# A recorded trunk issued in a planned order, and one product's weights summed by accumulating loads

## The chip, the cores and the metric

The kernel runs on one core of a Trainium2 chip. The metric is the time of one execution on the device in microseconds (us): the median of several runs. A core has five engines that run their own instruction streams in order: PE (TensorE, matrix products), DVE (VectorE), ACT (ScalarE), POOL (GpSimd) and SP (SyncE, which here only issues transfers). Streams wait for one another by semaphores. Weights come from HBM by DMA, issued by SP (plain loads) and POOL (loads that add to what is in the tile).

## The reference, cut to what matters

Two layers on 512 tokens of width 1024, all in float32:

```python
for i in range(DEPTH):                       # 2
    hn = rmsnorm(h, mix_norm_g[i])
    if i % N_MIXERS == 0:
        h = h + sgu_mixer(hn, ...)           # W_o (u * (W_s LN(v) + b)), u, v = gelu(hn @ w_in)
    else:
        h = h + retention(hn, positions, ...) # 4 heads: rotary q, k; decayed causal scores; gated by silu(g)
    h = h + swiglu(rmsnorm(h, ffn_norm_g[i]), ffn_w_gu[i], ffn_w_down[i])   # hidden width 2816
return rmsnorm(h, final_norm_g)
```

The work is matrix products: `hn @ w_in`, the gate/up and down products of both layers, the four heads' q, k, v, g, scores and values, and the two output projections.

## The kernel before, in words

Every float32 operand is kept as a high and a low half, and each product is three matmuls (`three`, L246 to L249). The halves are made when they are needed: ACT copies the high half (L216), DVE subtracts it to get the low half (L223). Weights are fetched by SP (`load`, L346) or, adding, by POOL (`add`, L349); where two or three blocks of a weight matrix have to be summed, either POOL's adding loads do it, or DVE adds raw tiles (`plus`, L377).

Nearly all large products go through `seven`, a scheme of seven products instead of eight on 2 x 2 blocks, named P1, P7, P6, Q4, P5, P2 and P3, in an order given by ORDER, LATER, FIRST or SPREAD. Each accumulates into a PSUM tile named X, Y or Z (W for P3 of the last unit). For which products POOL's adding loads make the summed weights is the argument `dma`; `onto` names products whose weights are made by adding one more block onto the tile of the product before.

A PSUM tile is 128 x 2 x 512 floats: two halves of 512 columns. There are four such tiles (`PS`, tags ps0 to ps3), handed out in turn. The last product, P3, is computed half by half: all matmuls of half c = 0, then `evac(p, acc, 0)`, then all matmuls of half c = 1, then `evac(p, acc, 1)`, so that half 0 can be read on DVE or ACT while half 1 is still being computed:

```python
            elif n == len(steps) - 1:
                for c in range(2):
                    with tc.issue_after(mm.ins) if apart and c == 1 else nullcontext():
                        for st_ in steps[-by_chunk:]:
                            mm = matmuls(p, *st_, c)
                    evac(p, acc, c)
```

The readers of such halves that this text names are: the products `s` and `he` of the gate/up units (L1036, DVE), the sums into the residual X (L527, DVE), the gated `ur` (L969, DVE) and `mx` (L988, DVE) of the first mixer, the scores times decay `s` (L1182, DVE), and on ACT the activated `v` (L837), the gate `sg` (L1214), the squares `osq` (L1232), the turned `z` (L1247), the copies `xr` (L704) and `s_dn` (L539). In sc, pv, v and the like the two parts of one tile are filled and read one after the other in the same way. A gate/up unit u of layer l has tiles X_gu, Y_gu and Z_gu; the projection of values and gates of a retention head has X_vg, Y_vg and Z_vg; dn is a down projection, so and ro the output projections.

The stages are: the first mixer (v, u, mix, so), feed-forward of layer 0 (gate/up units 0 to 5, dn0_0, dn0_1), retention (qk and vg of heads 0 to 3, scores sc, values pv, zT, ro), feed-forward of layer 1, and the final norm. The down projection that ends the kernel, dn1_1, is the last unit: `into_x(..., apart=True)`.

The rotary tables (cos and sin of the positions, `rotary_tables`, L852 to L898) are a long row of small DVE operations, stepped through in gate/up unit 2 of layer 0; they are used where head 0's q and k are rotated (L1099, L1100).

What sets the order of the work: `pipeline` runs a list of jobs and calls the preparing steps of later jobs some jobs ahead (FETCH, HIGH, PREP and so on). Below that, the framework's scheduler (`schedule_with_timeline_sim=True`) may move an instruction of any engine ahead of others when it puts the streams together, and it knows `issue_after` and `high_priority`. The semaphores that it puts in follow whole tiles.

## Time and profile before

| | |
|---|---|
| runs, median (lowest to highest of 3) | 1202.37 us (1201.17 to 1203.57) |
| the profiled execution, its own time | 1203.41 us |
| its span in the profile | 1201.7 us |
| DMA | 225.90 MB, mean 188 GB/s |
| granted TensorE clock, whole span | 0.996 |

Rows of groups read: line, engine, operation, out<-in, partitions x elements, count, then busy us and mean ns of one, then the idle time of the engine just before them and what ended most of it. A wait of PE names what PE waited for. Matmuls are pipelined: one of 512 columns is shown as 0.39 us, but they start every 0.23 us.

### The profile page before, as it was taken

How to read it: one execution, taken by the hardware profiler on the slowest of the kernel's cores; microseconds unless marked ns; L12 is line 12 of the kernel's file. 1: busy time of each engine (PE TensorE's matmuls, PEld its weight loads, DVE VectorE, ACT ScalarE, POOL GpSimd, SP SyncE). 2: the span in 40 equal slices, each digit the busy share in tenths (PEclk: the TensorE clock that was granted, in tenths of full speed). 3: DMA queues.
4: the chain of work that ended last, by engine and by line, in shares of the span. 5: the costliest groups of instructions: out<-in, count | busy, mean ns of one | idle time of the engine just before them, and what ended most of it. 6: DMA issues, size and time to landing. Idle time of an engine off the chain costs nothing.

```text
span 1201.7 us, 18455 instructions
## 1 busy us (share of the span) xinstructions
PE 1180.0 (98%) x7374; PEld 1067.4 (89%) x7374; DVE 960.9 (80%) x1143; ACT 664.6 (55%) x842; POOL 171.0 (14%) x151
## 2 busy tenths in 40 slices
PE   8999999999999999999999999999999999999997
PEld 7888899989999987988989898878899989999986
DVE  5587998899977789787885959879788896676897
ACT  5523775554444547555664656566565545535465
POOL 1000122121010130110201111220121210101210
PEclk9999999999999999999999999999999999999999
DMA  9912878898684898777677868877868887856892
GB/s 314 282 47 59 244 161 182 226 228 208 160 205 108 225 184 265 176 163 184 155 202 178 192 155 203 183 151 247 217 153 211 186 216 210 199 135 192 168 245 97
DMA packets 128167, 225.90 MB, mean 188 GB/s; under 512 B 7464, under 2 KB 30032, under 8 KB 128080
## 3 DMA queue, kind: packets, MB, share of 16 engines
q1 hardware_dynamic: 88848, 153.37, 38.6%
q0 software_dynamic: 38944, 70.81, 35.3%
q8 instruction: 58, 0.95, 0.3%
q10 hardware_dynamic: 288, 0.52, 0.1%
q14 instruction: 29, 0.24, 0.1%
HBM read 221.53 MB, written 2.10 MB: 186 GB/s over the span
## 4 chain that ended last, share of the span: by engine, by line
PE 85%; DMA 5%; issue 4%; DVE 2%; ACT 2%; POOL 1%; SPq 0%; DVEq 0%; POOLq 0%; ACTq 0%
PE X_gu L247 6%; PE X_gu L249 6%; PE X_gu L248 6%; DMA wr_gu_P<-in_ffn_w_gu 3%; PE Y_gu L249 3%; PE Y_gu L248 3%; PE Y_gu L247 3%; PE X_dn L247 3%; PE X_dn L248 3%; PE X_dn L249 3%; PE X_vg L247 2%; PE X_vg L248 2%; PE X_vg L249 2%; PE ps_v L247 1%; PE Y_dn L248 1%
## 5 line engine op out<-in xcount | busy, mean ns | idle before, releaser
L216 ACT ACTIVATE wh_gu_P<-wr_gu_P 128x1024 fp32r<-128x1024 f32 x132 | 135.3, 1053 | 87.6 <-DVE wr_gu_P L377 51.0
L223 DVE TENSOR_TENSOR wl_gu_P<-wr_gu_P,wh_gu_P 128x1024 fp32r<-128x1024 f32 x132 | 158.7, 1219 | 25.4 <-ACT wh_gu_P L216 25.1
L349 POOL DMA_DIRECT2D wr_gu_P<-in_ffn_w_gu x50 | 60.9, 1258 | 414.0 <-DVE wl_gu_P L223 196.2
L216 ACT ACTIVATE wh_dn_P<-wr_dn_P 128x1024 fp32r<-128x1024 f32 x72 | 69.1, 980 | 42.6 <-DMA wr_dn_P<-in_ffn_w_down 17.8
L223 DVE TENSOR_TENSOR wl_dn_P<-wr_dn_P,wh_dn_P 128x1024 fp32r<-128x1024 f32 x72 | 79.4, 1128 | 2.7 <-issue 1.1
L223 DVE TENSOR_TENSOR wl_vg_P<-wr_vg_P,wh_vg_P 128x1024 fp32r<-128x1024 f32 x48 | 57.8, 1217 | 14.5 <-ACT wh_vg_P L216 14.4
L349 POOL DMA_DIRECT2D wr_dn_P<-in_ffn_w_down x36 | 41.9, 1239 | 143.6 <-DVE wl_dn_P L223 46.6
L216 ACT ACTIVATE wh_vg_P<-wr_vg_P 128x1024 fp32r<-128x1024 f32 x48 | 49.2, 1055 | 22.8 <-DMA wr_vg_P<-in_ret_w_in 16.7
L349 POOL DMA_DIRECT2D wr_vg_P<-in_ret_w_in x26 | 31.5, 1248 | 207.5 <-DMA wr_vg_P<-in_ret_w_in 73.8
L247 PE MATMUL X_gu<-XH_f,wh_gu_P 128*128 128x256 f32 x176 | 50.6, 288 | 2.2 <-ACT xr_f L704 2.2
L247 PE MATMUL Z_gu<-XH_f,wh_gu_P 128*128 128x256 f32 x176 | 50.0, 284 | 1.4 <-DVE s L1051 1.4
L247 PE MATMUL X_gu<-xP5h_f,wh_gu_P 128*128 128x256 f32 x176 | 50.0, 284 | 0.9 <-ACT u L1026 0.9
L249 PE MATMUL Y_gu<-XH_f,wl_gu_Q 128*128 128x256 f32 x176 | 49.9, 284 | 0.8 <-DVE wl_gu_Q L223 0.8
L248 PE MATMUL X_gu<-XL_f,wh_gu_P 128*128 128x256 f32 x176 | 50.5, 287 | 0.0
L249 PE MATMUL X_gu<-XH_f,wl_gu_P 128*128 128x256 f32 x176 | 50.5, 287 | 0.0
L247 PE MATMUL X_gu<-xP6h_f,wh_gu_P 128*128 128x256 f32 x176 | 50.0, 284 | 0.2
L247 PE MATMUL Y_gu<-XH_f,wh_gu_Q 128*128 128x256 f32 x176 | 49.9, 284 | 0.0
L249 PE MATMUL Z_gu<-XH_f,wl_gu_P 128*128 128x256 f32 x176 | 49.9, 283 | 0.0
L248 PE MATMUL X_gu<-xP6l_f,wh_gu_P 128*128 128x256 f32 x176 | 49.8, 283 | 0.0
L249 PE MATMUL X_gu<-xP3h_f,wl_gu_P 128*128 128x256 f32 x176 | 49.8, 283 | 0.0
L248 PE MATMUL X_gu<-xP3l_f,wh_gu_P 128*128 128x256 f32 x176 | 49.8, 283 | 0.0
L249 PE MATMUL X_gu<-xP6h_f,wl_gu_P 128*128 128x256 f32 x176 | 49.8, 283 | 0.0
(643 smaller groups left out, 4284.5 us busy)
## 6 DMA issues: line engine op xcount, KB each, us to landing
wr_gu_P<-in_ffn_w_gu SPq DMA_DIRECT2D x110, 512.0 KB, 5.3
wr_gu_P<-in_ffn_w_gu POOLq DMA_DIRECT2D x50, 512.0 KB, 7.8
wr_dn_P<-in_ffn_w_down SPq DMA_DIRECT2D x50, 512.0 KB, 5.5
wr_vg_P<-in_ret_w_in SPq DMA_DIRECT2D x40, 512.0 KB, 5.8
wr_dn_P<-in_ffn_w_down POOLq DMA_DIRECT2D x30, 512.0 KB, 7.3
wr_vg_P<-in_ret_w_in POOLq DMA_DIRECT2D x26, 512.0 KB, 6.9
wr_ro_P<-in_ret_w_out SPq DMA_DIRECT2D x20, 512.0 KB, 4.8
wr_qk_P<-in_ret_w_in SPq DMA_DIRECT2D x15, 512.0 KB, 5.9
```

Source lines behind the costliest of these rows:

```text
L216: nc.scalar.activation(h, s, AF.Copy)
L223: nc.vector.tensor_tensor(l, s, f32(h), ALU.subtract)
L247: nc.tensor.matmul(o, ah, bh, start=start, stop=False, skip_group_check=True)
L248: nc.tensor.matmul(o, ah, bl, start=False, stop=False, skip_group_check=True)
L249: return nc.tensor.matmul(o, al, bh, start=False, stop=stop, skip_group_check=True)
L349: nc.gpsimd.dma_start(raw[p, 0, g, s][:, 0:nk, :], source(b, g, s, nk), accum_op=ALU.add)
```

## The change

The trunk's instructions are no longer given to the framework's scheduler. Stand-ins for the engines, the pools and the tiles (`EngineProxy`, `Pool`, `Virtual`, `View`) record each call in a list with an estimated length, and with the recorded calls that it must follow. `order_of` then plans all engines' work in time, and `emit` issues the calls in the order of their planned starts under `tc.manual_schedule()`, in which the framework keeps the order it is given and only puts the semaphores in. PE's operations are taken in recorded order as soon as they may run (the lowest number that is ready); DVE, ACT, POOL and SP take, of what may run, the one whose latest start is earliest (`late`, from a backward pass). `issue_after` and `high_priority` no longer do anything.

Which calls must follow which is kept in grains: 512 floats (`BANK`) for PSUM tiles, a 64th of a tile for the others. So, in the planner, a reader of half 0 of a PSUM tile has nothing to do with a matmul into half 1.

In the last unit P5 joins P7 in `dma`: its weights come in four pieces, each a plain load of one block (12) by SP and an adding load of another (11) by POOL, and the four sums on DVE with P1's raw tiles go.

```diff
+BANK = 512
+RESULT = 35
+TO_PE = 55
+HW_DMAS = 8
...
+class Virtual:
...
+        self.grain = BANK if psum else max(1, free // 64)
...
+class Recorder:
...
+    def add(self, engine, call, reads, writes, what, busy, took, table=None, kind=None, slow=0):
...
+                t, m = v.tile, v.mask()
+                for q, qm, qw in t.history:
+                    if q is not op and (w or qw) and qm & m:
+                        op.before.add(q)
...
+    def issue_after(self, ins):
+        return nullcontext()
+
+    def high_priority(self):
+        return nullcontext()
...
+def order_of(rec, report=None):
...
+                if e == "PE":
+                    op = min((o for o in queue[e] if can(o)), key=lambda o: o.n, default=None)
+                else:
+                    for o in queue[e]:
+                        if can(o):
...
+                            cost = o.late + (3 * TABLE if o.table and o.table != table else 0)
+                            if op is None or (cost, o.n) < best:
+                                op, best = o, (cost, o.n)
...
+    return sorted(ops, key=lambda o: (o.start, o.n))
+
+
+def emit(rec):
+    with rec.tc.manual_schedule():
+        for op in order_of(rec):
+            op.call()
...
-    nc = tc.nc
...
+    rec = Recorder(tc)
+    nc, tc = rec, rec
...
-            made = seven(name, w, groups, 0, T, A, evac, mid, look, order=order, dma=("P7",), onto=("P6", "Q4"), apart=apart,
+            made = seven(name, w, groups, 0, T, A, evac, mid, look, order=order, dma=("P7", "P5") if apart else ("P7",), onto=("P6", "Q4"), apart=apart,
...
     pipeline(jobs)
+    emit(rec)
```

All instructions of the changed kernel have one line, L333, in `record`, so they are told apart by their tiles. Three places show how the order moves. In the rows, names in brackets are semaphores that the instruction waits for, by the engine that raises them (`Activation` is ACT).

PE in gate/up unit 2 of layer 0, before: the end of half 0 of P3, then the first product of unit 3, then half 1.

```order
L249 MATMUL X_gu_2_2611<-xP3h_f_1811,wl_gu_2_P_0_2_2901 128x256
L247 MATMUL X_gu_3_3130<-XH_f_1264,wh_gu_3_P_0_0_2942 128x256 [waits PE_49,Activation_49]
L248 MATMUL X_gu_3_3130<-XL_f_1265,wh_gu_3_P_0_0_2942 128x256
...
L249 MATMUL X_gu_3_3130<-XH_f_1264,wl_gu_3_P_0_2_2973 128x256
L247 MATMUL Y_gu_3_3195<-xP7h_f_1542,wh_gu_3_P_0_0_3012 128x256 [waits PE_49,Activation_49]
L247 MATMUL X_gu_2_2611<-xP3h_f_1811,wh_gu_2_P_0_0_2867 128x256 [waits DVE_49]
```

The same place in the changed kernel: the end of half 0 (the first row), then half 1 at once.

```order
L333 MATMUL X_gu_2_2620<-xP3h_f_1730,wl_gu_2_P_0_2_2745 128x256
L333 MATMUL X_gu_2_2620<-xP3h_f_1730,wh_gu_2_P_0_0_2717 128x256
L333 MATMUL X_gu_2_2620<-xP3l_f_1746,wh_gu_2_P_0_0_2717 128x256
...
L333 MATMUL X_gu_2_2620<-xP3l_f_1746,wh_gu_2_P_0_0_2717 128x256
L333 MATMUL X_gu_2_2620<-xP3h_f_1730,wl_gu_2_P_0_0_2733 128x256 [waits DVE_49]
L333 MATMUL X_gu_2_2620<-xP3h_f_1730,wh_gu_2_P_0_2_2727 128x256
```

The 48 matmuls of unit 3 no longer stand between the halves. Half 1 begins without a wait, and its twelfth matmul waits for DVE. The DVE instruction that it waits for is the product `s` of half 0, which itself waits for PE: for the eleventh matmul of half 1, the one just ahead.

PE in the projection of values and gates of retention head 2, before: half 0 of X_vg ends, 26 other matmuls follow (X_qk of head 3, and two of the values pv of head 2), then half 1.

```order
L249 MATMUL X_vg_6516<-wh_vg_P_0_2_6696,xP3l_r 128x512
L247 MATMUL X_qk_6918<-XH_r,wh_qk_P_0_0_6715 128x256 [waits DVE_49,Activation_49]
...
L249 MATMUL X_qk_6918<-XH_r,wl_qk_P_0_0_6716 128x256
L247 MATMUL X_vg_6516<-wh_vg_P_0_0_6656,xP3h_r 128x512 [waits Activation_49]
L248 MATMUL X_vg_6516<-wl_vg_P_0_0_6657,xP3h_r 128x512
```

The same place in the changed kernel.

```order
L333 MATMUL X_vg_6512<-wh_vg_P_0_2_6633,xP3l_r 128x512
L333 MATMUL X_vg_6512<-wh_vg_P_0_0_6620,xP3h_r 128x512
L333 MATMUL X_vg_6512<-wl_vg_P_0_0_6630,xP3h_r 128x512
L333 MATMUL X_vg_6512<-wh_vg_P_0_0_6620,xP3l_r 128x512
L333 MATMUL X_vg_6512<-wh_vg_P_0_0_6620,xP3h_r 128x512 [waits Activation_49]
```

Again nothing stands between the halves, and the fourth matmul of half 1 waits for ACT's `sg` of half 0, which waits for the third.

DVE where retention starts, before: the norm of the last token blocks (`nf_dn`, `xs_r`), low halves of weights (`wl_vg`) and of the turned input (`XL_r`).

```order
L685 SCALAR_TENSOR_TENSOR xs_r_4891<-X,nf_dn_1_1_4884,g_r 128x1024 [waits DVE_49]
L223 TENSOR_TENSOR wl_vg_P_0_0_4836<-wr_vg_P_0_0_4812,wh_vg_P_0_0_4835 128x1024 [waits DMAHW2_49]
L223 TENSOR_TENSOR wl_vg_P_0_2_4895<-wr_vg_P_0_2_4832,wh_vg_P_0_2_4894 128x1024 [waits DMAHW4_49,Activation_49]
L672 TENSOR_TENSOR XL_r<-xT_r_4928,XH_r 128x8x128 [waits Activation_49]
L223 TENSOR_TENSOR wl_vg_P_0_0_4926<-wr_vg_P_0_0_4794,wh_vg_P_0_0_4925 128x1024 [waits DMASW7_49]
L672 TENSOR_TENSOR XL_r<-xT_r_5007,XH_r 128x8x128 [waits Activation_49]
```

The same stretch in the changed kernel, with steps of the rotary tables (`turn`, `frac`, `sum`, `turns`) among them.

```order
L333 SCALAR_TENSOR_TENSOR xs_r_4911<-X,nf_dn_1_1_4899,g_r 128x1024 [waits DVE_49]
L333 TENSOR_TENSOR XL_r<-xT_r_4872,XH_r 128x8x128 [waits PE_49,Activation_49]
L333 TENSOR_TENSOR sum_4935<-turns,frac_4902 128x512 [waits DVE_49]
L333 TENSOR_SCALAR turns_4943<-ahl 128x512
L333 CAST turn_4949<-sum_4935 128x512 [waits DVE_49]
L333 CAST turn_4954<-turns_4943 128x512 [waits DVE_49]
L333 TENSOR_TENSOR turns<-sum_4935,turn_4949 128x512 [waits DVE_49]
L333 TENSOR_TENSOR frac_4966<-turns_4943,turn_4954 128x512 [waits DVE_49]
L333 TENSOR_TENSOR XL_r<-xT_r_4938,XH_r 128x8x128 [waits PE_49,Activation_49]
```

The tables have moved to a place with nearly 200 us more of TensorE's work ahead of it, the stretch between the end of dn0_1 and head 0's scores.

## Prediction

> **What bounds the kernel now.** I read the page first, for its busy times.

> ```profile
> span 1201.7 us, 18455 instructions
> PE 1180.0 (98%) x7374; PEld 1067.4 (89%) x7374; DVE 960.9 (80%) x1143; ACT 664.6 (55%) x842; POOL 171.0 (14%) x151
> ```

> TensorE sets the time: it is busy for 1180.0 of 1201.7 us. The change takes no matmul away. It can only remove TensorE's waits, or add some. So the second view is the waits of PE (engine, line, what was waited for, total us, times, longest).

> ```profile
> PE xT_in L667 <- DMA X<-in_x: 2.2, 1, 2.2
> PE X_gu L247 <- ACT xr_f L704: 2.2, 1, 2.2
> PE X_ro L247 <- ACT z_P6h L502: 1.6, 1, 1.6
> PE Z_gu L247 <- DVE s L1051: 1.4, 1, 1.4
> PE wake L176 <- POOL eps L170: 1.2, 1, 1.2
> ...
> PE X_dn L247 <- ACT wh_dn_P L216: 0.5, 1, 0.5
> ```

> The whole list has 13 rows and adds up to 13.8 us. The rows of xT_in and wake (3.4 us) are the start of the kernel, which the change leaves alone; 10.4 us lie behind it. A little more hides in slow stretches after two of these waits. The timeline (start, duration, engine, line, operation, idle before and its releaser) has the waits, and the windows view (stretch, its length, busy time and count of PE, PEld, DVE, ACT and POOL, granted clock, DMA share, GB/s) what came 1 us later:

> ```profile
> 807.20 0.50 PE L247 MATMUL X_ro<-wh_ro_P,z_P6h 128*128 128x512 f32 x1 [1.60 <-ACT z_P6h L502]
> 808.45 0.50 PE L249 MATMUL X_ro<-wh_ro_P,z_P6l 128*128 128x512 f32 x1 [0.53 <-DVE z_P6l L506]
> ...
> 876.21 0.38 PE L247 MATMUL X_gu<-XH_f,wh_gu_P 128*128 128x256 f32 x1 [2.18 <-ACT xr_f L704]
> ```

> ```profile
> 808.80:812.30 3.50, 3.50 (x10) 2.71 (x9) 3.50 (x4) 2.97 (x4) 0.00 (x1) 0.52 1.10 272
> 877.20:880.60 3.40, 3.40 (x18) 3.40 (x18) 2.93 (x3) 3.39 (x4) 0.06 (x1) 0.50 0.02 5
> ```

> The granted clock is 0.52 and 0.50 for some 3.4 us each, so each stretch loses about 1.7 us, together 3.4. All that a better order could give behind the start is 10.4 + 3.4 = 13.8 us.

> **What the new order removes.** The places of the three longest waits are filled differently, and I take 12 of the 13.8 us as gained (bounds 6, if the new order keeps half of them, and 13.8).

> **What the new order adds: round trips.** A PSUM tile here has two halves, 512 columns each. In the last product of a group the code computes half 0, evacuates it on DVE or ACT, then computes half 1. The planner keeps its books in halves (BANK = 512): it lets half 1 start at once and puts the evacuation beside it, a few matmuls into half 1. The semaphores that the program is built with know only whole tiles. So the evacuation waits for the last matmul issued into the tile, the one just ahead, and the next matmul waits for the evacuation. TensorE stands still for a round trip. The scheduler of before puts other matmuls between the halves instead, 48 and 26 of them at the two places shown with the change. I counted such places in the order with its waits: a matmul that waits for an ACT or DVE instruction that itself waits for a matmul less than 1 us of TensorE work earlier. Before has 4, two of them in the first 5 us. After has 44, one in the start. That leaves 2 before, which are the Z_gu and X_vg waits of the list above, and 43 after. The two show what one costs.

> ```profile
> 164.70 0.28 PE L248 MATMUL Z_gu<-XL_f,wh_gu_P 128*128 128x256 f32 x1
> 164.81 0.28 PE L249 MATMUL Z_gu<-XH_f,wl_gu_P 128*128 128x256 f32 x1
> 165.13 1.22 DVE L1051 TENSOR_TENSOR s<-s,Z_gu 128x1024 f32<-128x1024 f32 x1 [0.45 <-PE Z_gu L249]
> 166.50 0.36 PE L247 MATMUL Z_gu<-XH_f,wh_gu_P 128*128 128x256 f32 x1 [1.41 <-DVE s L1051]
> 166.69 0.28 PE L248 MATMUL Z_gu<-XL_f,wh_gu_P 128*128 128x256 f32 x1
> ```

> ```profile
> 772.01 0.58 ACT L1214 ACTIVATE sg<-X_vg 128x512 f32<-128x512 f32 x1
> 772.64 0.50 PE L247 MATMUL X_vg<-wh_vg_P,xP3h_r 128*128 128x512 f32 x1 [0.95 <-ACT sg L1214]
> 772.98 0.39 PE L248 MATMUL X_vg<-wl_vg_P,xP3h_r 128*128 128x512 f32 x1
> 773.21 0.39 PE L249 MATMUL X_vg<-wh_vg_P,xP3l_r 128*128 128x512 f32 x1
> ```

> On DVE: the last matmul starts at 164.81, the reader 0.32 later, and 0.15 after the reader's 1.22 the next matmul starts. From start to start that is 1.69 where 0.12 is usual (164.70 to 164.81): 1.57 lost, which is the reader's 1.22 plus 0.35. The matmul after that starts 0.19 later, not 0.12. So one costs the reader plus 0.42. On ACT the matmul starts 0.05 after the reader's end (772.59 to 772.64), 0.10 sooner than after DVE, and the following one 0.34 later where 0.23 is usual (772.98 to 773.21). With the reader starting as above, that is the reader plus 0.36.

> The readers and their durations (mean ns) come from the groups by form:

> ```profile
> L1036 DVE SCALAR_TENSOR_TENSOR s<-X_gu,s 128x512 f32<-128x512 f32 x16 | 11.0, 688 | 21.4 <-PE X_gu L249 21.4
> L527 DVE TENSOR_TENSOR X<-X,X_ro 128x512 f32<-128x512 f32 x4 | 2.7, 685 | 2.5 <-PE X_ro L249 2.5
> L969 DVE TENSOR_TENSOR ur<-ps_u,R 128x512 f32<-128x512 f32 x8 | 5.2, 683 | 2.0 <-PE ps_u L249 2.0
> L988 DVE SCALAR_TENSOR_TENSOR mx<-mix,gains_cols,add_b 128x512 f32<-128x512 f32 x8 | 6.0, 747 | 6.6 <-PE mix L986 6.6
> L1182 DVE TENSOR_TENSOR s<-sc,dec 128x512 f32<-128x512 f32 x4 | 2.8, 690 | 4.3 <-PE sc L249 4.3
> L837 ACT ACTIVATE v<-ps_v,ry_n 128x512 f32<-128x512 f32 x8 | 4.9, 683 | 9.1 <-PE ps_v L249 9.1
> L1214 ACT ACTIVATE sg<-X_vg 128x512 f32<-128x512 f32 x8 | 4.7, 587 | 1.4 <-PE X_vg L249 1.3
> L1232 ACT ACTIVATE osq<-pv 128x512 f32<-128x512 f32 x16 | 9.5, 596 | 20.6 <-PE pv L249 20.6
> L1247 ACT ACTIVATE z<-zT,gains_cols 128x256 f32<-128x256 f32 x32 | 12.6, 476 | 20.6 <-PE zT L1245 20.6
> L704 ACT ACTIVATE xr_r<-xT_r 128x512 f32<-128x512 f32 x8 | 4.3, 598 | 0.0
> L539 ACT ACTIVATE s_dn<-X_dn 128x1024 f32<-128x1024 f32 x4 | 4.1, 1018 | 4.0 <-PE X_dn L249 4.0
> ```

> On DVE there are 25 places: 10 products s and he (0.688), 6 sums into X (0.685), 4 ur (0.683), 2 mx (0.747), 3 s (0.690), together 17.3 us of readers. With 25 x 0.42 = 10.5 that is 27.8. On ACT there are 18: 3 v (0.683), 3 sg (0.587), 6 osq (0.596), 2 z (0.476), 3 xr (0.598), one s_dn (1.018), together 11.2 us. With 18 x 0.36 = 6.5 that is 17.7. The sum is 45.5 us. Bounds: 0.8 each where the reader starts sooner than I read it (34), and the 1.41 of the first row for each (61).

> [...]

> **The rotary tables.** Their DVE work is 15 groups of rows, from

> ```profile
> L891 DVE TENSOR_TENSOR sum<-turns,frac 128x512 f32<-128x512 f32 x5 | 3.4, 685 | 0.0
> ...
> L859 DVE CAST ahl<-ang 128x512 fp32r<-128x512 f32 x1 | 0.4, 418 | 0.0
> ```

> to that; their busy times add up to 22.6 us. Before does it in gate/up unit 2; after does it where retention starts. The windows view of before there:

> ```profile
> 478.00:537.00 59.00, 58.00 (x354) 51.67 (x352) 46.82 (x55) 34.21 (x47) 11.05 (x9) 1.00 0.80 187
> ```

> 46.8 + 22.6 = 69.4 us for DVE in 59.0: up to 10.4 too much, which TensorE would wait for. Against that, some sums can be done later, and the stretch gets longer by three round trips of its own. I take 4 us, bounds 0 and 10.4.

> **The fifth product's weights.** In the last unit 4 DVE sums go (L377) and 4 accumulating loads come on POOL (L349).

> ```profile
> L377 DVE TENSOR_TENSOR wr_dn_P<-wr_dn_P,wr_dn_P 128x1024 f32<-128x1024 f32 x10 | 12.1, 1217 | 0.0
> ```

> That is 4.9 us less for DVE. On POOL, busy for 14% of the span, four issues more stand ahead of the unit's other accumulating loads. TensorE shows no wait for weights there, so I take 0; bounds -1, if a sum would have been late, and +2, if a sum by load lands late. Three more table loads on ACT, which is busy for 55% of the span, fall beside matmuls: 0; one that fell on a round trip would lengthen it, within the bounds above.

> **Sum.** 45.5 - 12 + 4 + 0, and 2 for one or two half-speed stretches after close pairs of round trips, is 39.5. The profiled execution took 1203.41 us, so 1243 by it; the median of the runs is 1.0 lower, so 1242.

> **The rivals.**

> A, faster: the halves are guarded by themselves, and the 43 places cost nothing. For it: the readers start beside half 1 by plan, in another half. Against it: the waits of the order name whole tiles, and the 772.64 row. Then 1202.4 - 12 + 0 to 4 gives about 1190 to 1194. It decides where fewer than some 11 of the 43 places cost their 1.06 us, since 11 x 1.06 = 12 eats the gain.

> B, slower still: DVE bounds the start of retention with the whole 10.4 us. For it: the order has the tables between the sums that TensorE waits for. Against: DVE has 12 us free in that stretch. Then 1242 + 6 = 1248.

> C, slower still: close pairs of round trips slow the clock. Idle of 1.60 and 0.53 within 1.3 us halved it for 3.4 us; 1.41 and 0.95 alone did not. After has about 8 pairs within 4 us (v1, ur, ps_u1, xT_r, and pv in three heads). At 1.7 each that is 14 more than none, 12 more than I count: 1254. [...]

> **How the numbers follow.** The forecast has 0.69, A 0.09, B 0.10, C 0.12. The range leaves out A and the far ends: from 1216 (34 for the round trips, 13.8 gained, 0 elsewhere make 1223, and a few of the 43 places may be covered) to 1262 (C and B together make 1260). Within 0.2%, about 2.4 us, a measurement of this kernel can't tell it from no change. Of A's 0.09, 0.07 is faster and 0.02 lands within that bound; everything else, 0.91, is slower.

> **What the next profile would show.** Right: PE waits of over 30 us in total, on DVE s and he, X, ur and ACT osq, sg, each 0.7 to 1.4 us and in the middle of a group; PE's busy time as before; idle before PE's matmul of half 1 rather than of a new tile. If C holds, rows of PE below clock 1 in the slices of the page. Wrong: no such waits and a time near 1190, then the halves are free; or the waits there, but the time lower, then the old kernel lost more than its list of waits shows.

## The result, and the profile after

The changed kernel takes 1259.62 us (median of 4 runs, 1256.75 to 1262.65), the kernel before beside it 1201.77. The ratio is 1.048, with a 95% interval of 1.045 to 1.051. That is 57.9 us slower, where 40 were forecast. The page of the changed kernel:

```profile
span 1260.9 us, 18483 instructions
PE 1196.8 (95%) x7374; PEld 1073.9 (85%) x7374; DVE 961.9 (76%) x1139; ACT 676.8 (54%) x845; POOL 175.2 (14%) x155
```

PE does the same 7374 matmuls, but it is busy 16.8 us longer and idle for more. The list of its waits, which added up to 13.8 us before, has 22 rows and 56.3 us now:

```profile
PE X_gu L333 <- DVE s L333: 9.9, 8, 4.4
PE X_gu L333 <- ACT s L333: 6.1, 2, 3.5
PE pv L333 <- ACT osq L333: 4.8, 6, 0.8
PE sc L333 <- DVE s L333: 4.6, 3, 3.0
PE X_ro L333 <- DVE X L333: 3.3, 2, 2.5
PE ps_u L333 <- DVE ur L333: 3.1, 4, 0.8
PE X_dn L333 <- DVE X L333: 2.8, 2, 2.0
...
PE X_gu L333 <- ACT u L333: 2.1, 1, 2.1
```

Most rows are readers of half a tile, with a longest wait of 0.8 us. Some have a longest of 2 to 4.4. So there are two kinds. The first, in gate/up unit 2 of layer 0, at the place whose order the change's section shows:

```profile
335.42 0.28 PE L333 MATMUL X_gu<-xP3h_f,wh_gu_P 128*128 128x256 f32 x1
335.54 0.28 PE L333 MATMUL X_gu<-xP3l_f,wh_gu_P 128*128 128x256 f32 x1
335.86 0.69 DVE L333 SCALAR_TENSOR_TENSOR s<-X_gu,s 128x512 f32<-128x512 f32 x1 [0.62 <-PE X_gu L333]
336.61 0.39 PE L333 MATMUL X_gu<-xP3h_f,wl_gu_P 128*128 128x256 f32 x1 [0.79 <-DVE s L333]
336.83 0.28 PE L333 MATMUL X_gu<-xP3h_f,wh_gu_P 128*128 128x256 f32 x1
```

The reader starts 0.32 us after the start of the last matmul, as forecast, and PE goes on 0.06 after its end. From start to start 1.07 us pass where 0.12 is usual.

The second kind, a little earlier:

```profile
302.74 0.28 PE L333 MATMUL Y_gu<-xP7h_f,wl_gu_P 128*128 128x256 f32 x1
303.64 1.06 ACT L333 ACTIVATE wh_gu_Q<-wr_gu_P 128x1024 fp32r<-128x1024 f32 x1 [4.45 <-DMA wr_gu_P<-in_ffn_w_gu]
304.60 1.01 ACT L333 ACTIVATE s<-X_gu 128x1024 f32<-128x1024 f32 x1
305.66 0.58 PE L333 MATMUL X_gu<-xP6h_f,wh_gu_P 128*128 128x256 f32 x1 [2.64 <-ACT s L333]
```

ACT stands for 4.45 us at the copy of a weight whose load has not landed. Behind it in ACT's order is the copy `s` that frees the tile X_gu, and PE waits for that. The same at 1049.9 us (3.50 us idle). At 958 to 963 us it goes by way of DVE: DVE stands for 3.84 us at the low half of that weight, which needs ACT's copy. Then the low half, the sum `y` and the product `s` that half 1 waits for follow one another without a gap:

```profile
958.60 1.06 ACT L333 ACTIVATE wh_gu_Q<-wr_gu_P 128x1024 fp32r<-128x1024 f32 x1 [7.00 <-DMA wr_gu_P<-in_ffn_w_gu]
959.56 1.04 ACT L333 ACTIVATE u<-u 128x1024 f32<-128x1024 f32 x1
959.69 1.23 DVE L333 TENSOR_TENSOR wl_gu_Q<-wr_gu_P,wh_gu_Q 128x1024 fp32r<-128x1024 f32 x1 [3.84 <-ACT wh_gu_Q L333]
960.83 1.22 DVE L333 SCALAR_TENSOR_TENSOR y<-y,u 128x1024 f32<-128x1024 f32 x1
961.97 0.68 DVE L333 SCALAR_TENSOR_TENSOR s<-X_gu,s 128x512 f32<-128x512 f32 x1
962.70 0.58 PE L333 MATMUL X_gu<-xP3l_f,wh_gu_P 128*128 128x256 f32 x1 [4.40 <-DVE s L333]
```

The loads behind these three copies are adding loads, issued by POOL at 295.0, 949.0 and 1038.9 us. From their issue to the start of the copy 8.6, 9.6 and 9.0 us pass.

The windows view (granted clock in the third column from the end) has a slow stretch behind six waits, of 2.05, 2.64, 3.03, 2.50, 4.40 and 3.50 us:

```profile
206.00:208.80 2.80, 2.80 (x16) 2.80 (x14) 2.80 (x3) 1.50 (x2) 1.48 (x2) 0.50 0.23 17
304.50:311.20 6.70, 5.54 (x26) 5.54 (x27) 4.72 (x4) 4.86 (x6) 2.44 (x2) 0.53 0.99 240
792.50:796.20 3.70, 3.70 (x11) 3.12 (x12) 0.56 (x1) 0.00 (x0) 1.22 (x1) 0.58 0.37 85
878.40:881.90 3.50, 3.40 (x8) 2.73 (x9) 2.47 (x5) 1.72 (x5) 0.00 (x0) 0.51 0.82 255
960.80:967.50 6.70, 4.80 (x23) 4.80 (x24) 4.90 (x6) 2.78 (x3) 1.21 (x1) 0.53 0.53 96
1048.40:1055.10 6.70, 5.20 (x24) 5.20 (x25) 4.72 (x4) 5.20 (x6) 2.42 (x2) 0.55 0.98 231
```

Nearly all of the loss can be counted in the rows of PE: the distance between the starts of two matmuls, less the usual distance for that form (0.227, 0.120 or 0.109 us). From 20 us on:

| lost, us | before | after |
|---|---|---|
| 43 round trips (before: none of these) | - | 49.0 |
| other waits over 0.3 us | 12.3 | 10.2 |
| slow clock, where PE was not waiting | 3.4 | 13.3 |
| the rest, such as the slower matmul behind a wait | 4.2 | 5.5 |
| sum | 19.9 | 78.0 |

Half the clock for 30.7 us makes 15.3 us, but for 4.0 of the 30.7 PE stood at a wait that is counted already. The first 20 us lose 7.8 and 7.9, and behind the last matmul lie 7.7 us in both. The sums differ by 58.1 us; the first matmul starts 1.1 us later (2.3 us after the start of the span instead of 1.2). Together that is the 59.2 us between the two profiled spans, where the medians differ by 57.9. Of the 43 round trips, 39 lose 36.4 (0.93 each); four lose 2.2 (512 us), 3.2 (792), 2.7 (878) and 4.6 (963).

### The profile page after: what moved, and what is told of

It is laid out like the page before. It is cut to its first block, busy times and chain, and to the rows that moved or that the text cites. A ratio compares the mean times of both kernels' runs of the same rounds, so it can differ in the third digit from the quotient of the medians.

```text
span 1260.9 us, 18483 instructions
## 1 busy us (share of the span) xinstructions
PE 1196.8 (95%) x7374; PEld 1073.9 (85%) x7374; DVE 961.9 (76%) x1139; ACT 676.8 (54%) x845; POOL 175.2 (14%) x155
## 5 line engine op out<-in xcount | busy, mean ns | idle before, releaser
L333 DVE TENSOR_TENSOR wl_gu_P<-wr_gu_P,wh_gu_P 128x1024 fp32r<-128x1024 f32 x132 | 158.9, 1221 | 64.0 <-ACT wh_gu_P L333 36.4
L333 ACT ACTIVATE wh_gu_P<-wr_gu_P 128x1024 fp32r<-128x1024 f32 x132 | 136.0, 1054 | 101.0 <-DMA wr_gu_P<-in_ffn_w_gu 39.6
L333 POOL DMA_DIRECT2D wr_gu_P<-in_ffn_w_gu x50 | 60.9, 1273 | 400.7 <-DVE wl_gu_P L333 180.6
L333 ACT ACTIVATE wh_dn_P<-wr_dn_P 128x1024 fp32r<-128x1024 f32 (+1 forms) x72 | 69.8, 984 | 61.9 <-PE X_gu L333 24.4
L333 DVE TENSOR_TENSOR wl_dn_P<-wr_dn_P,wh_dn_P 128x1024 fp32r<-128x1024 f32 (+1 forms) x72 | 80.7, 1132 | 14.0 <-PE X_gu L333 5.0
L333 POOL DMA_DIRECT2D wr_dn_P<-in_ffn_w_down x40 | 46.4, 1213 | 190.8 <-DMA wr_dn_P<-in_ffn_w_down 111.5
L333 DVE TENSOR_TENSOR wl_vg_P<-wr_vg_P,wh_vg_P 128x1024 fp32r<-128x1024 f32 x48 | 57.6, 1219 | 9.4 <-ACT wh_vg_P L333 8.3
L333 POOL DMA_DIRECT2D wr_vg_P<-in_ret_w_in x26 | 31.6, 1243 | 203.1 <-DVE wl_vg_P L333 58.7
L333 ACT ACTIVATE wh_vg_P<-wr_vg_P 128x1024 fp32r<-128x1024 f32 x48 | 48.8, 1060 | 18.4 <-DMA wr_vg_P<-in_ret_w_in 13.5
L333 PE MATMUL X_gu<-xP6h_f,wh_gu_P 128*128 128x256 f32 x176 | 52.7, 299 | 6.1 <-ACT s L333 6.1
L333 PE MATMUL X_gu<-xP3l_f,wh_gu_P 128*128 128x256 f32 x176 | 51.0, 290 | 6.8 <-DVE s L333 6.8
L333 PE MATMUL X_gu<-xP3h_f,wl_gu_P 128*128 128x256 f32 x176 | 51.0, 290 | 3.1 <-DVE s L333 3.1
L333 PE MATMUL X_gu<-xP5h_f,wh_gu_P 128*128 128x256 f32 x176 | 50.7, 288 | 2.1 <-ACT u L333 2.1
L333 PE MATMUL X_gu<-xP6h_f,wl_gu_P 128*128 128x256 f32 x176 | 52.2, 297 | 0.0
L333 PE MATMUL X_gu<-xP6l_f,wh_gu_P 128*128 128x256 f32 x176 | 52.2, 296 | 0.0
L333 PE MATMUL X_gu<-xP3h_f,wh_gu_P 128*128 128x256 f32 x176 | 50.6, 288 | 1.6 <-DVE he L333 1.6
L333 PE MATMUL X_gu<-xP5h_f,wl_gu_P 128*128 128x256 f32 x176 | 50.5, 287 | 0.0
L333 PE MATMUL X_gu<-xP5l_f,wh_gu_P 128*128 128x256 f32 x176 | 50.5, 287 | 0.0
L333 PE MATMUL Y_gu<-xP7h_f,wh_gu_P 128*128 128x256 f32 x176 | 50.0, 284 | 0.0
L333 PE MATMUL Y_gu<-xP7l_f,wh_gu_P 128*128 128x256 f32 x176 | 50.0, 284 | 0.0
L333 PE MATMUL X_gu<-XH_f,wh_gu_P 128*128 128x256 f32 x176 | 49.9, 284 | 0.0
L333 PE MATMUL Y_gu<-xP7h_f,wl_gu_P 128*128 128x256 f32 x176 | 49.9, 284 | 0.0
```

The source lines that it names most:

```text
L333: return fn(*[real_of(a) for a in args], **{k: real_of(a) for k, a in kwargs.items()})
```

## The experiments

Theory 1 was that of the prediction: the planner's halves make round trips. Theory 2 came from the trace after: loads land later than planned, and in a fixed order ACT and DVE stand behind them. Theory 3 was the rotary tables. The ratios are to runs of the kernel before on the same chip. Differences between two changed versions are of their medians, from chips on which the kernel before took between 1201.5 and 1202.1 us.

**Whole tiles in the planner.** The order is computed again, all else as changed:

```diff
-        self.grain = BANK if psum else max(1, free // 64)
+        self.grain = free if psum else max(1, free // 64)
```

> The changed kernel, but the planner keeps its books on PSUM by whole tiles instead of halves, so it plans other matmuls between the halves. Theory 1 (round trips inside a tile cost most of the loss): in the changed kernel the 43 places lose 49.0 us from start to start, 39 of them 36.4 us in all and four long ones 12.6, and the matmul behind each some 0.08 more. They go, so the time is 1259.6 - 36.4 - 3.5 = 1220 or less, down to 1205 if the four long ones and their slow clock go too. PE's list of waits has no row of a reader of half 0 over 1 us in total. Rival (the planned order loses by late loads and full queues, and the round trips only show slack that would be lost elsewhere): 1245 to 1260.

Measured: 1219.92 us (ratio 1.014, 1.011 to 1.017), 39.7 less than the changed kernel. The waits of PE:

```profile
PE X_gu L333 <- ACT s L333: 6.0, 2, 3.3
PE xT_f L333 <- DVE xs_f L333: 4.4, 3, 2.1
PE X_gu L333 <- ACT u L333: 3.4, 1, 3.4
...
PE sc L333 <- DVE s L333: 1.2, 1, 1.2
PE ps_v L333 <- ACT XH_in L333: 1.1, 1, 1.1
```

No matmul waits any more for osq, ur, mx, v, sg or he. The two waits behind late loads (ACT s) are still there with 6.0 us. Theory 1 holds at its forecast size, and it is not all. The 39.7 is a net figure: counted as in the table, 47.0 of the 49.0 us of round trips are gone, 9.8 us of waits at other places have come (for xs_f, nf_dn and s among them), and the slow clock takes 3.6 less. That it is so near the price of the 39 short round trips is in part luck.

**One kind of round trip put back.** Only the X tiles of the gate/up units are planned by halves:

```diff
+        self.grain = (BANK if name.startswith("X_gu") else free) if psum else max(1, free // 64)
```

> As the run with whole tiles, but the X tiles of the gate/up units are planned by halves again: 10 of the 43 round trips come back, all products s and he of 0.69 us. Theory 1: each costs 0.94 us, as measured in the changed kernel, so 9 to 11 us above the run with whole tiles. Rival: PE's waits there are only taken over from other places, within 3 us of it.

Measured: 1232.07 us (1.024, 1.021 to 1.027), 12.2 more than with whole tiles, a little more than the 9 to 11 expected. The ten places lose 17.6 us by the start-to-start count: eight 0.94 each, and two 4.8 and 5.2, where the reader was held up behind a late load. One of these takes the place of the wait for ACT u, 3.5 us.

**Loads planned to land 3 us later.**

```diff
-LAND = 2200
+LAND = 5200
```

> The changed kernel, but its planner reckons with 3 us more from a load's issue to its landing (LAND 5200, not 2200), so that it issues loads earlier and puts the copies that wait for them later in ACT's order. Theory 2 (loads that land later than planned hold up ACT, and behind it the reader that frees a PSUM tile: the waits at 306, 963 and 1050 us with 2.8, 4.6 and 3.7 us and a slow clock of 3.4 us lost in all after each): 13 to 20 us less, 1240 to 1247. If only the round trips matter: 1256 to 1263.

Measured: 1236.90 us (1.029, 1.026 to 1.031), 22.7 less than the changed kernel, a little beyond the range of theory 2. The view of cores, and the waits:

```profile
core 0: 1235.2 us, clock 0.999
```

```profile
PE X_gu L333 <- DVE s L333: 6.3, 8, 0.8
PE pv L333 <- ACT osq L333: 5.6, 7, 0.8
PE mix L333 <- DVE mx L333: 3.4, 4, 0.8
PE ps_u L333 <- DVE ur L333: 3.1, 4, 0.8
```

The round trips stay (46 of them, 0.94 us each), none is long any more, and the waits for ACT s and u are gone. The clock is 0.999, where it was 0.986. So the long waits and the slow clock go when the plan has loads land later, and 46 short waits, some close together, slow no clock. For the three waits at 306, 963 and 1050 us the trace after shows the late load itself. For the others it does not: the readers at 792 and 878 us end a row of DVE work without a gap, and at 206 ACT's copy waits for a DVE sum. That these go too is shown, but not by which way.

**Both.**

> Whole tiles and late loads together. If both theories hold and add up: 1198 to 1208, about the kernel before (1202). If late loads don't matter: the same as with whole tiles alone, within 3 us.

Measured: 1200.92 us (0.9990, 0.9978 to 1.0002). The two effects add up but for 4 us: 1259.6 - 39.7 - 22.7 = 1197. With both, the planned order is as fast as the old one. Its four largest rows of waits:

```profile
PE X_dn L333 <- ACT s_dn L333: 2.5, 2, 1.6
PE wake L333 <- POOL ones L333: 2.3, 1, 2.3
PE xT_f L333 <- DVE xs_f L333: 2.3, 1, 2.3
PE X_gu L333 <- DVE XL_f L333: 2.0, 1, 2.0
```

**Which loads are late.** The 3 us for adding loads alone, or for plain ones alone, at the three places where the planner uses LAND (`kind` is "add" or "load"):

```diff
-                    begin = max(now + op.busy + LAND - 300, dma_free)
+                    begin = max(now + op.busy + LAND + 3000 * (op.kind == "add") - 300, dma_free)
```

> The changed kernel (planner in halves), with 3 us more from issue to landing in the plan for adding loads alone. In the changed kernel ACT's copy in front of the three late readers (306, 963, 1050 us) is that of a Q weight, made by an adding load. If those alone are the late ones: as with all loads late, 1235 to 1239. If plain loads matter as much: about half of the 23 us, 1246 to 1252.

> The same for plain loads alone. If the adding loads alone are the late ones: 1256 to 1263, no change. If plain loads matter as much: 1246 to 1252.

Measured: 1236.97 us (1.029, 1.028 to 1.031) and 1241.92 us (1.033, 1.032 to 1.035). Adding loads alone bring all of it, as the first expectation says; plain loads alone bring 17.7 of 22.7, which fits neither. An adding load follows a plain load into the same tile, so time given to the plain one may move the other as well; that wasn't tried apart.

**More room for loads.** LAND 8200, with whole tiles.

> Whole tiles, with 6 us more from issue to landing in the plan (LAND 8200). If 3 us were not yet enough: 1196 to 1200. If 3 us were enough and earlier loads only hold buffers longer: 1201 to 1215.

Measured: 1199.97 us (0.9989, 0.9980 to 0.9999). No difference from 1200.92 that these runs can tell. 3 us were enough.

**The second part alone, in the old order.** The kernel before, with one line of the change:

```diff
+            made = seven(..., dma=("P7", "P5") if apart else ("P7",), ...)
```

> The kernel before, with only the second part of the change: in the last unit P5's weights are summed by adding loads. The forecast counted 0 for it (bounds -1 and +2): TensorE waits for no weights there and DVE is not what it waits for. So 1201 to 1204, no difference that can be measured. Rival (the adding loads land late and hold up ACT's copies): 2 to 4 us more, with PE waits on X_dn in the last 60 us.

Measured: 1203.65 us (1.0014, 1.0004 to 1.0023). That is 1.5 us, within the expectation and below the 0.2%.

**The second part left out, in the mended order.**

> Whole tiles and late loads, without the second part of the change (the sums on DVE as before). If the second part is worth nothing in a planned order either: within 2.5 us of 1200.9. If it takes work from a full DVE at the end: 3 to 5 us more than 1200.9 (4 sums of 1.22).

Measured: 1208.77 us (1.0055, 1.0043 to 1.0067), 7.9 more than with it. Neither number was right. The timeline of PE in the last unit shows where most of it goes:

```profile
1144.70 0.49 PE L333 MATMUL Z_dn<-wh_dn_P,h_P2h 128*128 128x512 f32 x1 [1.87 <-ACT h_P2h L333]
1146.16 0.79 PE L333 MATMUL Z_dn<-wl_dn_P,h_P2h 128*128 128x512 f32 x1 [0.96 <-DVE wl_dn_P L333]
1147.49 0.79 PE L333 MATMUL Z_dn<-wh_dn_P,h_P2l 128*128 128x512 f32 x1 [0.53 <-DVE h_P2l L333]
...
1153.95 0.50 PE L333 MATMUL Z_dn<-wl_dn_P,h_P2h 128*128 128x512 f32 x1 [1.61 <-DVE wl_dn_P L333]
```

These four waits aren't in the list of the run with the loads. They are 5.0 us, and a matmul that takes 0.79 where 0.39 is usual shows the clock behind them (0.74 granted on average from 1143 to 1156 us). The four sums themselves are not in the way. The first of them starts behind the waits, the others at 1168.5, 1169.6 and 1175.0:

```profile
1161.31 1.22 DVE L333 TENSOR_TENSOR wr_dn_P<-wr_dn_P,wr_dn_P 128x1024 f32<-128x1024 f32 x1
```

Ahead of the waits DVE works from 1123 to 1146 us without a gap, on low halves and sums of activations in another order than in the run with the loads. So leaving the loads out changed the plan ahead of them; why the planner then chose this order was not tried. In the old order, with the sums, PE has no such wait. Another 1.6 us of this profiled run is a slow stretch at 159 us, far from the last unit (see the last section).

**The rotary tables early.** In the changed kernel, and in the mended order:

```diff
     backward(ops, lazy, total, gap)
+    for op in ops:
+        if op.engine != "PE" and op.what.split()[-1].startswith(("pos", "ang", "ahl", "turn", "frac", "sum", "quarter", "CS")):
+            op.late -= 150000
```

> The changed kernel, with the rotary tables' operations wanted 150 us sooner by the planner, so that they come in gate/up units 2 and 3 again and not where retention starts. Theory 3 (the tables make DVE late there): of the waits at 512 us (2.2, of which a round trip is 0.9) and at 563 us (1.5), 2 to 3 us go: 1256 to 1258. Rival (what was late there is ACT's and DVE's order behind late loads): no difference from 1259.6 outside the spread of 3 us, and the two waits stay.

> Whole tiles, late loads and the tables early together. The run without the last has one wait of 0.6 us at the start of retention, so there is at most that to gain: 1199 to 1201.5. If the tables now take DVE time in the gate/up units that something needs there: 1202 to 1206.

Measured: 1260.58 us (1.049, 1.047 to 1.051) and 1200.48 us (0.9990, 0.9981 to 0.9998). Neither differs from its partner. In the first the wait for k0h where the scores begin is gone (1.5 us), and that for X in dn0_1 stays:

```profile
516.32 0.51 PE L333 MATMUL X_dn<-wl_dn_P,h_P3h 128*128 128x512 f32 x1 [1.81 <-DVE X L333]
```

The scatter of the changed kernel, 3 us either way, hides 1.5. So theory 3 is worth little more than that, and falls as a cause of most of what is seen.

The fastest versions, at 1200 us, are 0.1% below the kernel before, less than the 0.2% that a measurement here can tell.

## Why the prediction was right or wrong

- **What bounds the kernel.** Right: the same matmuls, and the difference shows as waits and slow matmuls of PE. The sign "PE's busy time as before" did not hold: it is 16.8 us longer. The slow clock, at which a matmul of 256 columns is busy for 0.41 us instead of 0.28, makes 9.9 of that by the table; the rest was not taken apart.
- **Round trips, 45.5 us.** Right, in place, number and price: 43 places, 39 of them at 0.93 each and some 0.10 for the matmul behind, where 1.06 was forecast. These 39 cost about 40. The order mended for the round trips alone gives back 39.7 net.
- **Four of the 43.** Not foreseen: they wait for a reader that is late itself, and lose 12.6 where 4 were counted. Where the plan has loads land 3 us later, none is longer than the rest.
- **What the new order removes, 12 us.** Mis-sized. All waits of before behind the start are gone (12.3 and 3.4 for the clock), but four others came, of 10.2 us: at 306 and 1050 us behind ACT's copies of late loads, at 206 behind a copy on ACT that waits for a sum on DVE, at 563 for k0h. Net it is 5.5. The step that failed is that an order without the old waits was taken for one without waits. For the two behind late loads the cause could be read ahead, from the code and from the page of before, whose DMA issues (KB each, median us from issue to landing) read

```profile
wr_gu_P<-in_ffn_w_gu SPq DMA_DIRECT2D x110, 512.0 KB, 5.3
wr_gu_P<-in_ffn_w_gu POOLq DMA_DIRECT2D x50, 512.0 KB, 7.8
```

 while the planner reckons 0.45 + 1.9 + 1.35 + 0.3 = 4.0 us for the first and 1.2 + 1.9 + 2.7 + 0.3 = 6.1 for the second, on a free queue.
- **Slow clock, 2 us.** Mis-sized: 13.3 in all, beside the waits. Rival C had nearly the right price (14) for a wrong reason. Close pairs of round trips did not slow the clock in these runs: it is 1.00 in this window of the changed kernel with two of 0.84 and 0.78 us idle,

```profile
588.00:594.00 6.00, 4.64 (x20) 3.56 (x21) 3.56 (x4) 3.94 (x9) 0.00 (x0) 1.00 0.75 138
```

 and 0.999 over a run with 46. Each slow stretch of the changed kernel stands behind one wait of 2.05 us or more. One wait of 2.02 us, at 511.5, has none behind it; the last section shows how it lay.
- **The rotary tables, 4 us, and rival B.** DVE is indeed full there, 58.0 of 62 us, but moving them away brings at most 1.5.

```profile
494.00:556.00 62.00, 58.60 (x364) 51.97 (x363) 58.00 (x96) 33.08 (x47) 9.76 (x8) 1.00 0.68 154
```

- **The fifth product's weights, 0.** Right in the old order (1.5 us). In the mended planned order they save 7.9, so the price depends on the order that is planned with or without them. In the changed kernel itself they were not tried.
- **Rival A.** Wrong: the readers wait for the matmul just ahead in the other half. This program's semaphores guard by tile: in gate/up unit 2 the reader of half 0 starts at 335.86 us, 0.32 after the start of the eleventh matmul into half 1, and PE goes on 0.06 after its end. And planning by tiles too is worth 39.7 us.

## What to carry to other kernels

A planner must use the same grain for dependences as the code that puts in the waits: planned finer than that, two parts that should run side by side become a round trip, here 0.93 us each. And a fixed order has to plan a load's landing no earlier than the trace shows it (in the page of before a median of 7.8 us for these adding loads, where 6.1 is reckoned): here ACT stood for 4.45 us at a copy whose load had not landed, the copy behind it in the order frees a PSUM tile, and PE waited 2.64 us for that one. What a change of one engine's load is worth has to be measured in the order in which it will run.

## What the hardware showed that was not expected

Two runs show side by side that nearly the same waits can leave the clock as it was or not. With whole tiles and late loads, and the same without the fifth product's loads, the lists of waits have 0.9 us (for ACT's XH_f) and 2.0 us (for DVE's XL_f) at the first gate/up unit. What came behind them, in this order:

```profile
157.90:161.30 3.40, 3.40 (x29) 3.40 (x30) 2.51 (x9) 3.40 (x8) 1.21 (x1) 1.00 1.05 245
158.70:162.10 3.40, 3.40 (x17) 3.40 (x17) 2.52 (x9) 3.40 (x8) 1.20 (x1) 0.50 1.05 248
```

In the traces of before and after a slow stretch took one step, 3.41 us, where PE stood idle for at most 0.1 us of that step, and two, 6.83 us, where it stood idle for 0.69 us or more of the first: in the changed kernel behind the waits of 2.64, 3.50 and 4.40 us. The matmuls of one step lost 1.4 to 1.7 us, those of two 2.0 to 2.8. So of two waits near 2 us in the changed kernel one cost nothing beside itself and the other 1.5 us more, by where they fell on the grid. That two versions of a kernel can differ by that much through luck is an estimate from these two.
